# Reading the moving operand of every main matmul as two halves in turn

## The chip, the cores and the metric

The kernel runs on one core of a Trainium2 chip. The metric is the time of one execution on the device in microseconds (us). TensorE (PE) multiplies, VectorE (DVE) and ScalarE (ACT) do the elementwise work, GpSimd (POOL) a few small things, and SyncE (SP) issues nearly all DMAs. A matmul has a stationary operand, which is loaded into TensorE first (a row "PEld" of the profile), and a moving operand, which is streamed through it column by column; its result lands in PSUM, in banks of 512 fp32 columns.

## What is computed

One layer of a hybrid decoder on x of 512 tokens by 2048 features, all in float32:

```python
h    = rms_norm(x, norm1_g);  proj = h @ w_in          # 2048 -> 6160 columns
out_a = gla_mixer(...)        # 4 heads of chunked gated linear attention
out_b = dilated_mixer(...)    # 8 heads of dilated attention, three branches merged
x = x + concat(out_a, out_b) @ w_out                   # 2048 -> 2048
h2 = rms_norm(x, norm2_g)
x = x + (silu(h2 @ w_gate) * (h2 @ w_up)) @ w_down     # 2048 -> 5632 -> 2048
```

The five big products (w_in, w_out, w_gate, w_up, w_down) hold nearly all the work. The mixers are small beside them.

## The kernel before, in words

**The big products.** The work goes by pairs: one pair multiplies 512 tokens by two weight blocks of 512 columns each. A pair uses a Strassen-like scheme of seven products (P1, P5, P6, P3, P7, P2, P4 in `PRODUCTS`) in place of eight, each over a quarter of the weights, and each product runs over `groups` of 256 rows (four, or three in the last third of w_down). So a pair with four groups is 28 items. `stream` (L302) walks all items of 20 pairs as one list; `first_pair` (L369) does the same for the first pair with a hand-written order of side work (`FIRST`).

For each item a weight sum of 128 x 1024 is made by DVE where the product needs one (`source`, L245), and split into a high part `wh` (ACT, L315, rounded to the type fp32r) and a low part `wl` (DVE, L319, the rest, fp32r). The activations were split in the same way into `a[:, :, 0, :]` and `a[:, :, 1, :]` (L174, L175). The product is high x high, low x high and high x low, so an item has 12 matmuls: 8 with `wh` as moving operand, 4 with `wl` (L345; L413 in the first pair). Each matmul streams `w[:, jj, :]`, 512 fp32r columns that lie next to each other in one partition (2048 bytes), against 128 x 128 of `a`, and adds into one bank `acc`. Two slots each of `wh` and `wl` (`hpool`) let the split of item k+1 run while item k is multiplied.

**Moves out of PSUM.** A product that is complete is read out of `acc` by ACT into a `seed` tile (`seeds`, L269 without and L271 with a row scale), or added from `acc` to such a tile by DVE (`close`, L281 and L283). In the first pair the two are L427 and L437. The last quarter of a pair is read straight out of PSUM by the pair's final step: `emitted` (L536), `final_gate` (L1128 and L1134), `residual` (L1293) or the silu in `final_ffn` (L1408). All read 512 neighbouring columns and write 512 neighbouring columns. `later(1, ...)` and `later(2, ...)` put them one and two items behind the end of the product, in the middle of an item's matmuls.

**What sets the order.** PE, ACT and DVE take their instructions in the order in which the code above issues them. The mixers, the transposes (L1092) and the splits of activations are generators in `background`, from which `step` runs a few between the `wh` and the `wl` matmuls of an item. The weights come by DMAs of 512 KB from SP (L222) into 12 slots.

Of the kernel before, what the change touches and what calls it, by code (L numbers as in the profile page):

```python
# [13 lines left out]
AF = mybir.ActivationFunctionType  # L14
ALU = mybir.AluOpType
# [3 lines left out]
P = 128  # L19
# [88 lines left out]
def block_kernel(ctx: ExitStack, tc: tile.TileContext, ins, out):  # L108
    nc = tc.nc
# [109 lines left out]
    def load_quarter(rows, name, g, w):  # L219
# [2 lines left out]
        load(t, w[r0 : r0 + 256, :].rearrange("(j p) n -> p j n", p=P))  # L222
        return t

    class Pair:


# [35 lines left out]
        def seeds(self, src, half):  # L263
            res = []

            def one(m):
                t = cpool.tile([P, 512], F32, name=nm("seed"), tag="C")
                if self.scale is None:
                    nc.scalar.copy(t, src[m])  # L269
                else:  # L270
                    nc.scalar.activation(t, src[m], AF.Copy, scale=self.scale(half, m))  # L271
                res.append(t)

            later(1, lambda: one(0))
            later(2, lambda: one(1))
            return res

        def close(self, seed, src, half, which):
            def one(m):
                if self.scale is None:  # L280
                    nc.vector.tensor_tensor(seed[m], src[m], seed[m], op=ALU.add)  # L281
                else:
                    nc.vector.scalar_tensor_tensor(  # L283
                        seed[m], src[m], self.scale(half, m), seed[m], op0=ALU.mult, op1=ALU.add
                    )
                if m == 1:
                    self.final(half, which, seed, None)

            later(1, lambda: one(0))
            later(2, lambda: one(1))  # L290
# [11 lines left out]
    def stream(pairs):  # L302


        items = [(p, prod, g) for p in pairs for prod in PRODUCTS for g in range(p.op.groups)]
        last = len(items) - 1
        sources, high, low = {}, {}, {}

        def total(k):
            p, prod, g = items[k]  # L310
            sources[k] = p.source(prod, g)

        def first_part(k):
            high[k] = hpool.tile([P, 2, 512], F32R, name=nm("wh"), tag="wh")
            nc.scalar.copy(high[k], sources[k])  # L315

        def second_part(k):
            low[k] = hpool.tile([P, 2, 512], F32R, name=nm("wl"), tag="wl")
            nc.vector.tensor_tensor(  # L319
                low[k], sources.pop(k), high[k].bitcast(F32), op=ALU.subtract  # L320
            )

        total(0)
        first_part(0)
        total(1)
        second_part(0)
        for k, (p, prod, g) in enumerate(items):
            if g == 0:
                if prod == "P1" and p.before:
                    p.before()  # L330
                p.begin(prod)
            run_soon()
            if k < last:
                first_part(k + 1)
            if k + 2 <= last:
                total(k + 2)
            if k < last:
                second_part(k + 1)
            a = p.op.t[COMBO[prod], g]
            fresh = prod in ("P1", "P5", "P2")  # L340
            for w, terms in ((high.pop(k), (0, 1)), (low.pop(k), (0,))):
                for jj in range(2):
                    for m in range(2):
                        for hl in terms:
                            nc.tensor.matmul(  # L345
                                p.dst[prod][m], a[:, jj, hl, m * P : (m + 1) * P], w[:, jj, :],
                                start=fresh and g == 0 and len(terms) == 2 and jj == 0 and hl == 0,
                                stop=g == p.op.groups - 1 and len(terms) == 1 and jj == 1,
                                skip_group_check=not fresh,
                            )  # L350
                if len(terms) == 2:
                    p.step()
            if g == p.op.groups - 1:
                p.end(prod)
# [14 lines left out]
    def first_pair(op, rows, w1, w2, final, unit, pre):  # L369
# [36 lines left out]
        def multiply(k, w, terms):  # L406
            prod, g = items[k]
            fresh = prod in ("P1", "P2", "P5", "P4")
            a = op.t[COMBO[prod], g]
            for jj in range(2):  # L410
                for m in range(2):
                    for hl in terms:
                        recent["pe"] = nc.tensor.matmul(  # L413
                            dst[prod][m], a[:, jj, hl, m * P : (m + 1) * P], w[:, jj, :],
                            start=fresh and g == 0 and len(terms) == 2 and jj == 0 and hl == 0,
                            stop=g == op.groups - 1 and len(terms) == 1 and jj == 1,
                            skip_group_check=not fresh,
                        ).ins

        seeds = {}  # L420

        def seed(name):
            prod, half = {"a": ("P1", 0), "b": ("P5", 1), "c": ("P1", 0), "d": ("P1", 1)}[name]
            seeds[name] = []
            for m in range(2):
                t = cpool.tile([P, 512], F32, name=nm("seed"), tag="C")
                recent["act"] = nc.scalar.activation(  # L427
                    t, dst[prod][m], AF.Copy, scale=row_scale(half, m)
                ).ins
                seeds[name].append(t)  # L430

        def close(name):
            prod, half, which = {
                "a": ("P2", 0, 0), "c": ("P5", 0, 1), "b": ("P1", 1, 1), "d": ("P4", 1, 0)
            }[name]
            for m in range(2):
                recent["dve"] = nc.vector.scalar_tensor_tensor(  # L437
                    seeds[name][m], dst[prod][m], row_scale(half, m), seeds[name][m],
                    op0=ALU.mult, op1=ALU.add,
                ).ins  # L440
            final(half, which, seeds[name], None)
# [89 lines left out]
    def emitted(c, scale):  # L531

        res = []
        for m in range(2):
            t = cpool.tile([P, 512], F32, name=nm("cout"), tag="C")
            nc.scalar.activation(t, c[m], AF.Copy, scale=scale(m))  # L536
            res.append(t)
        return res

# [115 lines left out]
    for what in LOADS.split():  # L655
        name, i = what[0], int(what[1])
# [461 lines left out]
    def final_gate(half, which, tiles, acc_):  # L1118
        og = onorm.pop((half, which))
        if tiles is None:  # L1120
            tiles = [cpool.tile([P, 512], F32, name=nm("cr"), tag="C") for _ in range(2)]
            src = acc_
        else:
            src = tiles
        for m in range(2):
            if src is acc_:
                nc.vector.scalar_tensor_tensor(
                    og[m], src[m], row_scale(half, m), og[m], op0=ALU.mult, op1=ALU.mult  # L1128
                )
                neg = nrs1[:, 2 * half + m : 2 * half + m + 1]  # L1130
            else:
                nc.vector.tensor_tensor(og[m], src[m], og[m], op=ALU.mult)
                neg = -1.0
            nc.scalar.activation(tiles[m], src[m], AF.Exp, scale=neg)  # L1134
            nc.scalar.activation(tiles[m], tiles[m], AF.Ln, bias=1.0)
            nc.scalar.activation(tiles[m], tiles[m], AF.Exp, scale=-1.0)

        def rest():
            for m in range(2):
                nc.vector.tensor_tensor(tiles[m], tiles[m], og[m], op=ALU.mult)  # L1140
            spare = apool.tile([P, 2, 2, 256], F32, name=nm("turned"), tag="A")
            later(1, lambda: transposed_store(
                tiles, half, mix_d[2 * which : 2 * which + 2], spare=spare
            ))

        soon(rest, 2)
# [141 lines left out]
    def residual(tiles, acc_, rest):  # L1288
        res = []
        for m in range(2):  # L1290
            r = rest[m]
            if tiles is None:
                nc.vector.tensor_tensor(r, acc_[m], r, op=ALU.add)  # L1293
                res.append(r)
            else:
                nc.vector.tensor_tensor(tiles[m], tiles[m], r, op=ALU.add)
                res.append(tiles[m])
        return res
# [98 lines left out]
    def final_ffn(j):  # L1397
        ups = {}

        def final(half, which, tiles, acc_):  # L1400
# [4 lines left out]
            for m in range(2):  # L1405
                if tiles is None:
                    s = work(("q", "k")[m])
                    nc.scalar.activation(s, acc_[m], AF.Silu, scale=tok_scale(half, m))  # L1408
                else:
                    s = tiles[m]  # L1410
                    nc.scalar.activation(s, s, AF.Silu)
                nc.vector.tensor_tensor(up[m], up[m], s, op=ALU.mult)
# [151 lines left out]
```

## Time and profile before

| what | us |
|---|---|
| median of 3 runs (2044.23 to 2045.43) | 2045.07 |
| the profiled execution | 2045.94 |
| its span, first to last instruction | 2044.1 |
| PE busy (9226 matmuls) | 2012.2 |
| DVE busy (1850 instructions) | 1657.6 |
| ACT busy (1600 instructions) | 1101.2 |
| POOL busy | 58.1 |

A row of the grouped view has the line of the kernel, the engine, the operation, output and inputs by the program's names, the shape and the count, then the busy time of the group in us and the mean of one instruction in ns, then the idle time of the engine just before them and what ended it. Busy times of matmuls overlap, since one starts before the one ahead has ended; so the mean of one matmul is not the distance between two.

### The profile page before, as it was taken

How to read it: one execution, taken by the hardware profiler on the slowest of the kernel's cores; microseconds unless marked ns; L12 is line 12 of the kernel's file. 1: busy time of each engine (PE TensorE's matmuls, PEld its weight loads, DVE VectorE, ACT ScalarE, POOL GpSimd, SP SyncE). 2: the span in 40 equal slices, each digit the busy share in tenths (PEclk: the TensorE clock that was granted, in tenths of full speed). 3: DMA queues.
4: the chain of work that ended last, by engine and by line, in shares of the span. 5: the costliest groups of instructions: out<-in, count | busy, mean ns of one | idle time of the engine just before them, and what ended most of it. 6: DMA issues, size and time to landing. Idle time of an engine off the chain costs nothing.

```text
span 2044.1 us, 25815 instructions
## 1 busy us (share of the span) xinstructions
PE 2012.2 (98%) x9226; PEld 1661.4 (81%) x9226; DVE 1657.6 (81%) x1850; ACT 1101.2 (54%) x1600; POOL 58.1 (3%) x81
## 2 busy tenths in 40 slices
PE   7999999999999999999999999999999999999999
PEld 6888888887877777888888888888888888888887
DVE  7997786768689889868868768778779979979977
ACT  7664464566675775544544444445446645546443
POOL 0000131011000000000000000000000000000000
PEclk9999999999999999999999999999999999999999
DMA  8347455454666684453453553543545855855662
GB/s 268 131 160 240 132 164 174 136 153 141 211 204 229 201 278 153 140 180 127 157 173 122 164 157 122 165 157 122 170 152 170 273 195 177 295 173 174 234 206 72
DMA packets 237113, 360.45 MB, mean 176 GB/s; under 512 B 18246, under 2 KB 96783, under 8 KB 236984
## 3 DMA queue, kind: packets, MB, share of 16 engines
q1 hardware_dynamic: 236776, 358.72, 54.0%
q8 instruction: 72, 1.18, 0.2%
q14 instruction: 57, 0.47, 0.1%
q10 hardware_dynamic: 208, 0.08, 0.0%
HBM read 296.59 MB, written 64.51 MB: 177 GB/s over the span
## 4 chain that ended last, share of the span: by engine, by line
PE 88%; DVE 5%; DMA 4%; issue 1%; ACT 1%; SPq 1%; POOL 0%; DVEq 0%; ACTq 0%; POOLq 0%
PE acc L345 79%; PE acc L413 3%; DVE wl L319 2%; PE bank L1092 1%; DVE wa L245 1%; PE bank L989 1%; PE bank L957 1%; DMA x<-in_x 1%; DVE AS L175 1%; PE bank L982 0%; DMA top<-mix_d 0%; DMA xn_d<-oT 0%; DMA wc<-in_w_in 0%; PE bank L413 0%; PE bank L742 0%
## 5 line engine op out<-in xcount | busy, mean ns | idle before, releaser
L345 PE MATMUL acc<-wh,AS 128*128 128x512 f32 x3008 | 745.1, 390 | 0.0
L345 PEld LDWEIGHTS acc<-wh,AS 128*128 128x128 f32 x3008 | 565.1, 188 | 118.6 <-ACT wh L315 0.3
L315 ACT CAST wh<-wa 128x1024 fp32r<-128x1024 f32 x376 | 395.9, 1053 | 453.3 <-PE acc L345 421.1
L345 PE MATMUL acc<-wh,AA 128*128 128x512 f32 x2256 | 558.0, 389 | 1.4 <-ACT wh L315 1.4
L319 DVE TENSOR_TENSOR wl<-wa,wh 128x1024 fp32r<-128x1024 f32 x376 | 458.2, 1220 | 105.0 <-ACT wh L315 64.9
L345 PEld LDWEIGHTS acc<-wh,AA 128*128 128x128 f32 x2256 | 423.2, 188 | 90.0 <-ACT wh L315 2.0
L345 PE MATMUL acc<-wl,AS 128*128 128x512 f32 x1504 | 410.3, 394 | 4.6 <-DVE wl L319 4.5
L345 PEld LDWEIGHTS acc<-wl,AS 128*128 128x128 f32 x1504 | 280.5, 188 | 67.5 <-DVE wl L319 8.5
L345 PE MATMUL acc<-wl,AA 128*128 128x512 f32 x1128 | 309.1, 395 | 2.0 <-DVE wl L319 2.0
L345 PEld LDWEIGHTS acc<-wl,AA 128*128 128x128 f32 x1128 | 209.1, 188 | 45.4 <-DVE wl L319 3.1
L315 ACT CAST wh<-wb 128x1024 fp32r<-128x1024 f32 x94 | 99.1, 1054 | 130.2 <-PE acc L345 123.4
L315 ACT CAST wh<-wc 128x1024 fp32r<-128x1024 f32 x94 | 99.0, 1053 | 127.8 <-PE acc L345 112.6
L315 ACT CAST wh<-wd 128x1024 fp32r<-128x1024 f32 x94 | 99.1, 1054 | 116.5 <-PE acc L345 111.6
L319 DVE TENSOR_TENSOR wl<-wc,wh 128x1024 fp32r<-128x1024 f32 x94 | 114.8, 1222 | 50.3 <-ACT wh L315 47.9
L319 DVE TENSOR_TENSOR wl<-wd,wh 128x1024 fp32r<-128x1024 f32 x94 | 114.7, 1221 | 47.9 <-ACT wh L315 40.7
L245 DVE TENSOR_TENSOR wa<-wc,wa 128x1024 f32<-128x1024 f32 x94 | 114.5, 1223 | 42.6 <-DMA wc<-in_w_gate 24.0
L319 DVE TENSOR_TENSOR wl<-wb,wh 128x1024 fp32r<-128x1024 f32 x94 | 114.4, 1219 | 10.7 <-ACT wh L315 10.2
L245 DVE TENSOR_TENSOR wb<-wd,wb 128x1024 f32<-128x1024 f32 x94 | 114.6, 1219 | 0.5
L245 DVE TENSOR_TENSOR wa<-wb,wa 128x1024 f32<-128x1024 f32 x94 | 113.7, 1220 | 0.8
L245 DVE TENSOR_TENSOR wa<-wd,wa 128x1024 f32<-128x1024 f32 x94 | 112.9, 1219 | 0.1
L283 DVE SCALAR_TENSOR_TENSOR seed<-acc,rs,seed 128x512 f32<-128x512 f32 x96 | 70.5, 747 | 29.5 <-PE acc L345 29.5
L271 ACT ACTIVATE seed<-acc,rs 128x512 f32<-128x512 f32 x96 | 60.6, 681 | 1.3 <-PE acc L345 1.2
(283 smaller groups left out, 1368.5 us busy)
## 6 DMA issues: line engine op xcount, KB each, us to landing
wa<-in_w_gate SPq DMA_DIRECT2D x44, 512.0 KB, 3.5
wb<-in_w_up SPq DMA_DIRECT2D x44, 512.0 KB, 4.3
wd<-in_w_up SPq DMA_DIRECT2D x44, 512.0 KB, 3.4
wc<-in_w_gate SPq DMA_DIRECT2D x44, 512.0 KB, 3.4
wc<-in_w_in SPq DMA_DIRECT2D x28, 512.0 KB, 3.8
wa<-in_w_in SPq DMA_DIRECT2D x24, 512.0 KB, 4.4
wb<-in_w_in SPq DMA_DIRECT2D x24, 512.0 KB, 6.0
wd<-in_w_in SPq DMA_DIRECT2D x24, 512.0 KB, 5.6
```

The source lines that it names most:

```text
L175: nc.vector.tensor_tensor(a[:, :, 1, :], src, a[:, :, 0, :].bitcast(F32), op=ALU.subtract)
L245: nc.vector.tensor_tensor(src, self.quarter(one, g), src, op=ALU.subtract)
L271: nc.scalar.activation(t, src[m], AF.Copy, scale=self.scale(half, m))
L283: nc.vector.scalar_tensor_tensor(seed[m], src[m], self.scale(half, m), seed[m], op0=ALU.mult, op1=ALU.add)
L315: nc.scalar.copy(high[k], sources[k])
L319: nc.vector.tensor_tensor(low[k], sources.pop(k), high[k].bitcast(F32), op=ALU.subtract)
L345: nc.tensor.matmul(p.dst[prod][m], a[:, jj, hl, m * P : (m + 1) * P], w[:, jj, :], start=fresh and g == 0 and len(terms) == 2 and jj == 0 ...
L413: recent["pe"] = nc.tensor.matmul(dst[prod][m], a[:, jj, hl, m * P : (m + 1) * P], w[:, jj, :], start=fresh and g == 0 and len(terms) == 2 ...
L957: nc.tensor.matmul(lp[:, :n], qh[:, b * P : (b + 1) * P], kh[:, :n], start=True, stop=True)
L989: nc.tensor.matmul(op, vh[:, k, :], lgs[b][:, k * P : (k + 1) * P], start=(k == 0), stop=(k == b))
L1092: nc.tensor.transpose(bk[:, jj, m * P : (m + 1) * P], tiles[m][:, f : f + P], ident)
```

## The change

Each main matmul gets its moving operand through a view that takes column 0 of the first half, column 0 of the second half (256 columns, 1024 bytes further on), column 1 of the first half, and so on. The matmul still writes 512 neighbouring columns of `acc`, which now hold the two halves interleaved. Each move out of `acc` reads it in steps of two columns, first the even ones, then the odd ones, and writes them as two halves, so that every tile in SBUF is what it was. In `final_gate` the Exp is issued apart for the case that reads PSUM and the case that reads SBUF; the instructions are the same. Nothing else is changed: transposes, the mixers' matmuls, `wh`, `wl`, `a` and all DMAs are as before.

```diff
+    def folded(w):
+        return w.rearrange("p (b a) -> p a b", b=2)
+    def unfolded(t):
+        return t.rearrange("p (a b) -> p b a", b=2)
+    def halves(t):
+        return t.rearrange("p (b a) -> p b a", b=2)
...
-                    nc.scalar.copy(t, src[m])
+                    nc.scalar.copy(halves(t), unfolded(src[m]))
                 else:
-                    nc.scalar.activation(t, src[m], AF.Copy, scale=self.scale(half, m))
+                    nc.scalar.activation(
+                        halves(t), unfolded(src[m]), AF.Copy, scale=self.scale(half, m)
+                    )
...
-                    nc.vector.tensor_tensor(seed[m], src[m], seed[m], op=ALU.add)
+                    nc.vector.tensor_tensor(
+                        halves(seed[m]), unfolded(src[m]), halves(seed[m]), op=ALU.add
+                    )
                 else:
                     nc.vector.scalar_tensor_tensor(
-                        seed[m], src[m], self.scale(half, m), seed[m], op0=ALU.mult, op1=ALU.add
+                        halves(seed[m]), unfolded(src[m]), self.scale(half, m), halves(seed[m]),
+                        op0=ALU.mult, op1=ALU.add,
                     )
...
                             nc.tensor.matmul(
-                                p.dst[prod][m], a[:, jj, hl, m * P : (m + 1) * P], w[:, jj, :],
+                                p.dst[prod][m], a[:, jj, hl, m * P : (m + 1) * P], folded(w[:, jj, :]),
...
-            nc.scalar.activation(t, c[m], AF.Copy, scale=scale(m))
+            nc.scalar.activation(halves(t), unfolded(c[m]), AF.Copy, scale=scale(m))
...
-                nc.vector.tensor_tensor(r, acc_[m], r, op=ALU.add)
+                nc.vector.tensor_tensor(halves(r), unfolded(acc_[m]), halves(r), op=ALU.add)
...
-                    nc.scalar.activation(s, acc_[m], AF.Silu, scale=tok_scale(half, m))
+                    nc.scalar.activation(
+                        halves(s), unfolded(acc_[m]), AF.Silu, scale=tok_scale(half, m)
+                    )
```

The matmul, the seed and the close of the first pair (L413, L427, L437) and the two reads of PSUM in `final_gate` (L1128, L1134) are changed in the same manner.

More of the change, by code (lines that the diff above doesn't have):

```diff
@@ L413, in multiply @@
                         recent["pe"] = nc.tensor.matmul(
-                            dst[prod][m], a[:, jj, hl, m * P : (m + 1) * P], w[:, jj, :],
+                            dst[prod][m], a[:, jj, hl, m * P : (m + 1) * P], folded(w[:, jj, :]),
                             start=fresh and g == 0 and len(terms) == 2 and jj == 0 and hl == 0,
@@ L427, in seed @@
                 recent["act"] = nc.scalar.activation(
-                    t, dst[prod][m], AF.Copy, scale=row_scale(half, m)
+                    halves(t), unfolded(dst[prod][m]), AF.Copy, scale=row_scale(half, m)
                 ).ins
@@ L437, in close @@
                 recent["dve"] = nc.vector.scalar_tensor_tensor(
-                    seeds[name][m], dst[prod][m], row_scale(half, m), seeds[name][m],
+                    halves(seeds[name][m]), unfolded(dst[prod][m]), row_scale(half, m),
+                    halves(seeds[name][m]),
                     op0=ALU.mult, op1=ALU.add,
@@ L1127, in final_gate @@
                 nc.vector.scalar_tensor_tensor(
-                    og[m], src[m], row_scale(half, m), og[m], op0=ALU.mult, op1=ALU.mult
+                    halves(og[m]), unfolded(src[m]), row_scale(half, m), halves(og[m]),
+                    op0=ALU.mult, op1=ALU.mult,
                 )
                 neg = nrs1[:, 2 * half + m : 2 * half + m + 1]
+                nc.scalar.activation(halves(tiles[m]), unfolded(src[m]), AF.Exp, scale=neg)
             else:
                 nc.vector.tensor_tensor(og[m], src[m], og[m], op=ALU.mult)
-                neg = -1.0
-            nc.scalar.activation(tiles[m], src[m], AF.Exp, scale=neg)
+                nc.scalar.activation(tiles[m], src[m], AF.Exp, scale=-1.0)
             nc.scalar.activation(tiles[m], tiles[m], AF.Ln, bias=1.0)
```

## The prediction

> **What bounds the kernel now.** I read the page first: the span, the busy shares, the granted clock.
>
> ```profile
> span 2044.1 us, 25815 instructions
> PE 2012.2 (98%) x9226; PEld 1661.4 (81%) x9226; DVE 1657.6 (81%) x1850; ACT 1101.2 (54%) x1600; POOL 58.1 (3%) x81
> PEclk9999999999999999999999999999999999999999
> PE 88%; DVE 5%; DMA 4%; issue 1%; ACT 1%; SPq 1%; POOL 0%; DVEq 0%; ACTq 0%; POOLq 0%
> ```
>
> The clock is full from end to end, and PE carries 88% of the chain that ended last. A busy PE need not be PE at its best, so I read next how far apart the main matmuls start: a piece of that chain (start, length, what) in the middle of the feed-forward part, and one pair of the same part by engine.
>
> ```profile
> 1315.71 65.30 PE acc L345 x288
> ...
> 1237.65:1315.71 78.06, 78.06 (x354) 64.66 (x353) 60.35 (x59) 37.28 (x43) 0.00 (x0) 1.00 0.46 149
> ```
>
> 288 matmuls of 512 columns in 65.30 us are **0.2267 us from start to start**. The second row (stretch, length, then busy time of PE, PEld, DVE, ACT, POOL, clock, DMA share, GB/s) has PE busy in all of its 78.06 us, DVE in 60.35, ACT in 37.28. PE's stream is the bound, and DVE has 17.7 us to spare per pair. The groups by form show how many matmuls the change touches, and how little PE waits ahead of them.
>
> ```profile
> L345 PE MATMUL acc<-wh,AS 128*128 128x512 f32 x3008 | 745.1, 390 | 0.0
> L345 PE MATMUL acc<-wh,AA 128*128 128x512 f32 x2256 | 558.0, 389 | 1.4 <-ACT wh L315 1.4
> L345 PE MATMUL acc<-wl,AS 128*128 128x512 f32 x1504 | 410.3, 394 | 4.6 <-DVE wl L319 4.5
> L345 PE MATMUL acc<-wl,AA 128*128 128x512 f32 x1128 | 309.1, 395 | 2.0 <-DVE wl L319 2.0
> ...
> L413 PE MATMUL acc<-wh,AS 128*128 128x512 f32 x128 | 31.6, 389 | 0.0
> L413 PE MATMUL acc<-wl,AS 128*128 128x512 f32 x64 | 17.1, 390 | 0.0
> L413 PE MATMUL acc<-wh,AA 128*128 128x512 f32 x64 | 16.0, 392 | 0.7 <-ACT wh L393 0.7
> ...
> L413 PE MATMUL bank<-wh,AA 128*128 128x512 f32 x32 | 9.3, 440 | 0.0
> L413 PE MATMUL acc<-wl,AA 128*128 128x512 f32 x32 | 9.0, 402 | 0.0
> L413 PE MATMUL bank<-wl,AA 128*128 128x512 f32 x16 | 4.8, 426 | 0.0
> ```
>
> That is 7896 of L345 and 336 of L413, **8232 matmuls**; at 0.2267 us they are 1866 us of the span. PE idles 8.0 us ahead of those of L345. So the price of this change is 8232 times what one matmul's start-to-start time changes by: each 10 ns is 82 us.
>
> **The change part by part.** Count and order of the instructions stay on every engine, so no queue is passed and no wait is added. Two things change: how a matmul reads its moving operand, and how 352 moves read PSUM.
>
> *The moving read.* No row of the trace has a moving operand whose neighbours in the stream are not neighbours in memory, so the cost is bounded from both sides. The nearest rows for a slower stream are fp32 matmuls of the same 512 columns (line 822): each call shows as two records, and their columns have the same four bytes as fp32r ones.
>
> ```profile
> 179.97 1.02 PE L822 MATMUL bank<-T,mats 128*128 128x512 f32 x2
> ...
> L822 PE MATMUL bank<-T,mats 128*128 128x512 f32 x8 | 4.1, 594 | 0.0
> ```
>
> The first row (start, length, count) has two of them in 1.02 us, and one takes 0.594; the second starts 1.02 - 0.594 = **0.426 us** behind the first. That is twice 0.213, so an fp32r stream runs at about two columns in the time of one fp32 column. I read this as two neighbouring columns being fetched at once, a supposition that fits the factor but that no row proves. If it holds, a stream whose next column lies 1024 bytes away gets one column per fetch. The start-to-start time is then 0.426 at the least (the fp32 rate), and twice 0.2267 = 0.453 at the most (all that a matmul costs now is doubled). Below, the bound is a stream with nothing lost, half of 0.426 = 0.213. I take the slow side, because the fp32 row is the only one in which four-byte columns come one at a time, and there the middle, 0.440:
>
> 8232 x (0.440 - 0.2267) = 1756 us more. The 8.0 us of idling of L345 go away, as wh and wl get nearly twice the time. From the profiled execution, 2045.94: 2045.94 + 1756 - 8 = **3794 us**. Its ends: 8232 x 0.1993 = 1641 gives 3679, and 8232 x 0.2267 = 1866 gives 3904. The profiled execution stands 0.9 us above the median of the runs; that is nothing here.
>
> [...]
>
> *The moves out of PSUM.* They are these groups, with rows for the price of a column behind them:
>
> ```profile
> L283 DVE SCALAR_TENSOR_TENSOR seed<-acc,rs,seed 128x512 f32<-128x512 f32 x96 | 70.5, 747 | 29.5 <-PE acc L345 29.5
> L271 ACT ACTIVATE seed<-acc,rs 128x512 f32<-128x512 f32 x96 | 60.6, 681 | 1.3 <-PE acc L345 1.2
> L281 DVE TENSOR_TENSOR seed<-acc,seed 128x512 f32<-128x512 f32 x48 | 32.4, 686 | 13.7 <-PE acc L345 13.7
> L269 ACT COPY seed<-acc 128x512 f32<-128x512 f32 x48 | 25.6, 585 | 0.0
> ...
> L962 DVE CUSTOM_DVE_ANT_0 L<-bank,T 128x512 f32<-128x512 f32 x4 | 2.7, 687 | 1.3 <-PE bank L957 1.3
> L962 DVE CUSTOM_DVE_ANT_0 L<-bank,T 128x256 f32<-128x256 f32 x4 | 1.7, 420 | 0.3 <-PE bank L957 0.3
> ...
> L992 ACT COPY r<-bank 128x128 f32<-128x128 f32 x16 | 4.2, 265 | 1.8 <-PE bank L989 1.7
> ```
>
> DVE has 96 + 48 of them plus 6 (L437), 16 (L1293) and 2 (L1128), 168; ACT has 96 + 48 plus 8 (L427), 8 (L536), 22 (L1408) and 2 (L1134), 184. No row reads PSUM in steps. Below, the cost is nothing. Above, I let each column cost twice: DVE pays (687 - 420) / 256 = 1.04 ns a column, 0.53 us for 512, and ACT (585 - 265) / 384 = 0.83 ns, 0.43 us; together 168 x 0.53 = 90 us on DVE and 184 x 0.43 = 78 us on ACT. A gain is excluded, as the same columns are moved. In the forecast all of it is hidden: at 0.440 an item of 12 matmuls takes 5.3 us where it took 2.7, and DVE kept up with the old one. I take nothing. If that cover is gone, because PE keeps its pace, the cost is the first rival's.
>
> *Banks.* A bank is read one or two items behind the end of its product and written again by PE a product later, some 28 matmuls or 6 us on; a move longer by 0.5 us fits in.
>
> **The rivals.**
>
> *PE keeps its pace (the interleaved read costs nothing).* Then the change does nothing to what bounds the kernel, and only the slower moves are left. The place is DVE's queue in an item that has a close, a split of activations and a sum besides `wl`: the next `wl` comes late, and PE waits.
>
> ```profile
> PEld acc L345 <- DVE wl L319: 11.6, 14, 1.9
> PE acc L345 <- DVE wl L319: 6.5, 9, 1.5
> 1627.00:2044.00 417.00, 412.14 (x1821) 341.11 (x1819) 354.95 (x373) 201.83 (x237) 0.00 (x0) 1.00 0.57 190
> ```
>
> Such waits are few now (18.1 us in 23 waits), but DVE is 85% busy in the last 417 us. Of the 90 us I let 0 to 40 come through: 2046 to 2086, with 2055 as its point. Against it speaks that fp32r needs twice the rate of fp32.
>
> *Faster.* A matmul takes 0.2267 where the doubled fp32 rate gives 0.213; 13.7 ns are lost each time. If they are lost where a contiguous read goes on to the next stretch of memory, two streams in turn may cover each other's change, provided both halves can be held open at once; from there on it decides. All gone: 8232 x 0.0137 = 113 us, 1933; half gone: 1989. I price it at 1960. Matmuls of 256 columns speak against it:
>
> ```profile
> 60.58 2.04 PE L742 MATMUL bank<-AS,gs 128*128 128x256 f32 x16
> ...
> L742 PE MATMUL bank<-AS,gs 128*128 128x256 f32 x16 | 2.0, 280 | 0.0
> ```
>
> 16 of them in 2.04 us, the last 0.280 long, are (2.04 - 0.28) / 15 = 0.117 apart, 10.8 ns over half of 0.213. A loss per column would be half of 13.7; this is most of it, so the loss looks more like one per matmul, which no order of columns removes. [...]
>
> *A rate between.* The read loses something, but part of the pairing survives or the two fetches overlap: 0.25 to 0.41 us, 2240 to 3550.
>
> *A quarter of the pace.* If a column from elsewhere takes not one but two fetch times, 0.88 us: 2045.94 + 8232 x 0.653 = 7420. Nothing in the trace asks for it; nothing excludes it.
>
> **How the numbers follow.**
>
> | case | us | chance |
> |---|---|---|
> | half the pace (forecast) | 3679 to 3904, 3794 | 0.48 |
> | PE keeps its pace | 2046 to 2086, 2055 | 0.14 |
> | faster | 1933 to 2040, 1960 | 0.18 |
> | a rate between | 2240 to 3550 | 0.11 |
> | a quarter of the pace | about 7420 | 0.09 |
>
> The predicted time is the forecast's, 3794. The likeliest case's own range is 3680 to 3905. Both signs have weight, so the range that should hold 8 in 10 reaches down to the faster case: 1945 to 3905; left out are the quarter pace and the outermost of the faster case and of the forecast. About 0.2% is what a measurement of this kernel can tell from no change (2041 to 2049): 0.05 of the 0.14 in which PE keeps its pace falls there. So faster 0.18, same 0.05, slower 0.77.
>
> **What would show it.** In the profile after, the piece of 288 matmuls in the chain should take 288 x 0.440 = 127 us, within 123 to 131, and the mean of one main matmul should rise from 390 ns to about 600, as the 594 of the fp32 row. ACT's wait of `wh` for PE should roughly double, DVE's share fall from 81% towards 45%, and PE's idling ahead of L345's successor vanish. L283's and L269's means tell the cost of the stepped read of PSUM, 747 and 585 if there is none, about 1280 and 1010 if each column costs double. The prediction is wrong if the 288 matmuls take 65 us or less: then the supposition that neighbours are fetched together is wrong, and the sign hangs on whether they take 61 to 62 us (the loss per matmul goes) or 65.3 with DVE late.

## The result, and the profile after

The changed kernel takes 1985.3 us (median of 4 runs, 1983.05 to 1986.54) against 2045.25 for the kernel before: a ratio of 0.970, 95% interval 0.9679 to 0.9721. It is **faster by 60 us**, where the forecast was 3794. From the page of the profile after:

```profile
span 1984.0 us, 25786 instructions
PE 1931.4 (97%) x9226; PEld 1672.0 (84%) x9226; DVE 1653.4 (83%) x1850; ACT 1096.3 (55%) x1600; POOL 62.4 (3%) x81
```

PE's busy time fell by 80.8 us; its idle time, span less busy, rose from 31.9 to 52.6 us, so 20.7 came back. The mean granted clock is 0.994 where it was 0.998. A piece of the chain of waits (start, length, what) and one feed-forward pair by engine:

```profile
1129.35 62.19 PE acc L361 x288
...
1129.35:1203.65 74.30, 74.30 (x353) 65.01 (x353) 60.19 (x59) 37.13 (x43) 0.00 (x0) 1.00 0.50 156
```

288 matmuls take 62.19 us where they took 65.30: **0.2159 us from start to start** in place of 0.2267. A pair is 74.30 us in place of 78.06, and DVE has 14.1 us to spare in it. The groups by form, two of the stream and the moves out of PSUM:

```profile
L361 PE MATMUL acc<-wh,AS 128*128 128x512 f32 x3008 | 714.0, 380 | 0.0
L361 PE MATMUL acc<-wh,AA 128*128 128x512 f32 x2256 | 536.0, 380 | 6.6 <-ACT wh L331 6.6
...
L298 DVE SCALAR_TENSOR_TENSOR seed<-acc,rs,seed 128x512 f32<-128x512 f32 x96 | 70.7, 749 | 24.7 <-PE acc L361 24.7
L282 ACT ACTIVATE seed<-acc,rs 128x512 f32<-128x512 f32 x96 | 60.8, 683 | 1.1 <-PE acc L361 1.0
L294 DVE TENSOR_TENSOR seed<-acc,seed 128x512 f32<-128x512 f32 x48 | 32.6, 692 | 11.7 <-PE acc L361 11.7
L280 ACT COPY seed<-acc 128x512 f32<-128x512 f32 x48 | 25.7, 589 | 0.0
```

The mean of a main matmul is 380 ns where it was 390 and 389. The moves out of PSUM take 749, 683, 692 and 589 ns where they took 747, 681, 686 and 585: the stepped read of PSUM costs under 1% in each of these groups.

So the sum is: 8232 x 10.8 ns = 89 us gained, 60 kept, 29 given back: 20.7 as idle time of PE, and some 8 because PE's busy time fell by 80.8 us and not by 89. Two questions were left: why a read that leaves its neighbours each time is faster, and where the 29 us went.

### The profile page after: what moved, and what is told of

It is laid out like the page before. It is cut to its first block, busy times and chain, and to the rows that moved or that the text cites. A ratio compares the mean times of both kernels' runs of the same rounds, so it can differ in the third digit from the quotient of the medians.

```text
span 1984.0 us, 25786 instructions
## 1 busy us (share of the span) xinstructions
PE 1931.4 (97%) x9226; PEld 1672.0 (84%) x9226; DVE 1653.4 (83%) x1850; ACT 1096.3 (55%) x1600; POOL 62.4 (3%) x81
## 4 chain that ended last, share of the span: by engine, by line
PE 83%; DVE 6%; DMA 6%; issue 2%; ACT 1%; SPq 1%; POOL 1%; DVEq 0%; ACTq 0%; POOLq 0%
PE acc L361 75%; PE acc L429 3%; DVE wl L335 2%; PE bank L1109 1%; DVE wa L256 1%; PE bank L1006 1%; PE bank L974 1%; DMA xn_d<-oT 1%; DMA x<-in_x 1%; ACT wh L331 1%; DMA x_d<-q 1%; DVE AS L175 1%; PE bank L999 0%; DMA wc<-in_w_in 0%; PE bank L759 0%
## 5 line engine op out<-in xcount | busy, mean ns | idle before, releaser
L361 PE MATMUL acc<-wh,AS 128*128 128x512 f32 x3008 | 714.0, 380 | 0.0
L361 PE MATMUL acc<-wh,AA 128*128 128x512 f32 x2256 | 536.0, 380 | 6.6 <-ACT wh L331 6.6
L361 PEld LDWEIGHTS acc<-wh,AA 128*128 128x128 f32 x2256 | 427.9, 190 | 68.6 <-ACT wh L331 7.8
L361 PE MATMUL acc<-wl,AS 128*128 128x512 f32 x1504 | 395.9, 385 | 7.9 <-DVE wl L335 7.8
L361 PE MATMUL acc<-wl,AA 128*128 128x512 f32 x1128 | 298.8, 387 | 3.6 <-DVE wl L335 3.4
```

Of the source, the lines that this page charges most:

```text
L361: nc.tensor.matmul(p.dst[prod][m], a[:, jj, hl, m * P : (m + 1) * P], folded(w[:, jj, :]), start=fresh and g == 0 and len(terms) == 2 and ...
```

## The experiments

### Which part does it: the reads alone, the moves alone

```diff
 # moves only: the changed kernel, but
-  ... a[:, jj, hl, m * P : (m + 1) * P], folded(w[:, jj, :]),
+  ... a[:, jj, hl, m * P : (m + 1) * P], w[:, jj, :],
 # reads only: the kernel before, but
-  ... a[:, jj, hl, m * P : (m + 1) * P], w[:, jj, :],
+  ... a[:, jj, hl, m * P : (m + 1) * P], folded(w[:, jj, :]),
```

> Only the moves out of PSUM are changed; the matmuls read neighbours, so the columns of what is moved come out permuted. If the gain is in the matmul's read: 2045, within 0.2% (L283 stayed at 747 to 749 ns in the profile after, so the stepped read of PSUM costs nothing). Rival, the gain is in the moves: 1985.

> Only the matmuls read the two halves in turn; the moves read neighbours, so the columns come out permuted. If the gain is in the matmul's read and the moves cost nothing: 1985, within 0.3% of the changed kernel. Rival, the moves give some of it back: 1975 or less. Rival, the gain is in the moves: 2045.

The moves alone: 2045.23 us, ratio 0.9997 (0.9988 to 1.0006), no change. The reads alone: 1980.13, ratio 0.9683 (0.9669 to 0.9698). The whole gain is in the matmuls' reads. To tell whether the reads alone are 5 us ahead of the whole change, both ran beside each other on one chip:

> The changed kernel once more, beside the next run on the same chip: 1983 to 1987.

> The reads alone once more (columns come out permuted): if the stepped moves out of PSUM cost something on the path, 4 to 6 us below the changed kernel, with intervals apart; if the first difference was scatter, within 2 us of it.

1981.82, ratio 0.9688 (0.967 to 0.9707), for the whole change and 1983.08, ratio 0.9686 (0.9671 to 0.9701), for the reads alone: the 5 us were scatter, and the stepped moves cost nothing that these runs can tell. The kernel before took 2046.52 us here, so the change is worth 64.7 us in this comparison and 60 in the first; the 29 us given back are 24 to 29.

### Is it any read that leaves its neighbours: steps of two

```diff
 def folded(w):
-    return w.rearrange("p (b a) -> p a b", b=2)   # column 0 of each half, column 1 of each half, ...
+    return w.rearrange("p (a b) -> p b a", b=2)   # columns 0, 2, 4, ..., then 1, 3, 5, ...
```

> As the run with the reads alone, but each matmul reads its even columns, then its odd ones (steps of two columns, 8 bytes); the columns come out permuted. Theory 'step': 1985, main matmuls 0.216 apart. Theory 'stretch': between 2030 and 2045, main matmuls 0.222 to 0.227 apart, since two sweeps of 256 pass over the same stretches one after the other.

3861.06 us, ratio 1.888 (1.8848 to 1.8911). Both theories named in the expectation fail. A piece of the chain:

```profile
1502.27 129.92 PE acc L349 x288
```

0.451 us from start to start. This is the half pace of the forecast, in size too (0.426 to 0.453), but for another order of the columns. Two orders, neither with a neighbour behind a neighbour, lie a factor of two apart (0.2159 and 0.451).

### The orders by themselves

A kernel that computes nothing of the layer and runs groups of 48 matmuls back to back, each line with its own order of the moving columns, for instance

```python
mm(o, stat(sr, i), wr[:, i // 4 % 2, :])                                      # L42, neighbours
mm(o, stat(sr, i), wr[:, i // 4 % 2, :].rearrange("p (b a) -> p a b", b=2))   # L43, halves in turn
```

> No part of the layer is computed: 24 groups of 48 matmuls, back to back, each group with its own order of the moving columns or its own type; read is the time from start to start. All theories: fp32r neighbours 0.227 us, two halves in turn 0.216. Theory 'stretch' (a contiguous fp32r read loses time at each new stretch of memory, and two streams far apart cover it): quarters and sixteenths in turn 0.216 too, halves 2048 bytes apart 0.216, but streams 2 or 16 columns apart, pairs or 16 columns in turn, and two runs of 256 neighbours stay at 0.220 to 0.227; a stationary operand with columns in steps of two changes nothing; 384 columns lose 10 ns (a share), not 13.7. Theory 'step' (what matters is only that the next column isn't the neighbour): every order whose next column is no neighbour gives 0.216, steps of two and the 2-column distance with it; runs and pairs stay near 0.227. Theory 'load' (the moving read collides with the load of the next stationary operand): stepped stationary columns change the 0.227, and 384 columns lose the full 13.7. fp32 and bf16 are not paired, or not limited by bytes: both orders alike, 0.43 a record and about 0.216. My old supposition (neighbours fetched together) would have had the halves at 0.43 or more and is out.

The timeline of PE (start, length, line, count); start to start is (length - mean of one) / 47, with the means from the second view. L42 is neighbours, L43 halves in turn, L44 quarters, L46 steps of two, L49 pairs of neighbours from each half in turn, L51 the order with distance 16 within blocks of 32, L52 the order 0,2,1,3, L54 two halves 2048 bytes apart; L61 and L62 are fp32 neighbours and halves, L63 and L64 bf16 neighbours and halves (the first record of L63 is missing from the trace, so its sum divides by 46).

```profile
19.41 11.04 PE L42 MATMUL bank<-wr,sr 128*128 128x512 f32 x48
30.29 10.52 PE L43 MATMUL bank<-wr,sr 128*128 128x512 f32 x48
40.65 13.75 PE L44 MATMUL bank<-wr,sr 128*128 128x512 f32 x48
...
75.08 21.85 PE L46 MATMUL bank<-wr,sr 128*128 128x512 f32 x48
...
139.70 16.50 PE L49 MATMUL bank<-wr,sr 128*128 128x512 f32 x48
...
167.56 10.52 PE L51 MATMUL bank<-wr,sr 128*128 128x512 f32 x48
177.92 11.05 PE L52 MATMUL bank<-wr,sr 128*128 128x512 f32 x48
...
199.69 10.52 PE L54 MATMUL bank<-wr,sr 128*128 128x512 f32 x48
210.05 11.36 PE L55 MATMUL bank<-wr,sr 128*128 128x512 f32 x48
...
258.86 41.37 PE L61 MATMUL bank<-w,s 128*128 128x512 f32 x96
300.06 52.00 PE L62 MATMUL bank<-w,s 128*128 128x512 f32 x96
352.12 10.31 PE L63 MATMUL bank<-wb,sbf 128*128 128x512 bf16 x47
362.26 23.41 PE L64 MATMUL bank<-wb,sbf 128*128 128x512 bf16 x48
```

```profile
L64 PE MATMUL bank<-wb,sbf 128*128 128x512 bf16 x48 | 23.4, 646 | 0.0
...
L46 PE MATMUL bank<-wr,sr 128*128 128x512 f32 x48 | 21.8, 633 | 0.0
...
L44 PE MATMUL bank<-wr,sr 128*128 128x512 f32 x48 | 13.7, 451 | 0.0
...
L42 PE MATMUL bank<-wr,sr 128*128 128x512 f32 x48 | 11.0, 389 | 0.0
...
L43 PE MATMUL bank<-wr,sr 128*128 128x512 f32 x48 | 10.5, 379 | 0.0
```

The kernel's own two times come out: (11.04 - 0.389) / 47 = 0.2266 for neighbours and (10.52 - 0.379) / 47 = 0.2158 for halves. Quarters are (13.75 - 0.451) / 47 = 0.283, steps of two (21.85 - 0.633) / 47 = 0.451; by the same sum pairs in turn are 0.340, and of the groups not shown here sixteenths are 0.435, 32 places in turn 0.433, steps of four 0.461, runs of 16 columns from each half in turn 0.240, and two runs of 256 one behind the other 0.227. Distance 16 and the halves 2048 bytes apart are as fast as the halves; 0,2,1,3 is as slow as neighbours. fp32 and bf16 **lose** by the same halves: 0.429 to 0.540 a record, and 0.216 to (23.41 - 0.646) / 47 = 0.484. So "stretch" falls (distance 16 should not have helped, quarters should have), and "step" falls (steps of two). Stepped stationary columns (L55) raise the neighbours' time to 0.233 and leave the halves at 0.216, as "load" had it; its other sign, that 384 columns lose the full 13.7 ns, did not come (11.5).

What fits these fp32r rows is a picture inferred from the times alone; no row of a trace shows a reader. The stream runs as if it were fetched by **two readers, one for the columns in even places of the order, one for those in odd places**, and as if what counts were how each reader's own columns lie. With halves in turn, one reader would get columns 0, 1, 2, ... and the other 256, 257, 258, ..., each a contiguous stream (0.2158). With neighbours each would get every second column (0.2266), with steps of two every fourth (0.451). With quarters and with pairs in turn each would jump between two places (0.283 and 0.340). fp32 and bf16 fit it with one reader, which jumps already with halves (0.540 and 0.484). The picture says which orders are slower; how much a jump costs (0.283, 0.340, 0.435) it doesn't say.

### The two readers put to a test

> No part of the layer is computed: 23 groups of 48 matmuls as in the first bench. New theory 'two readers': an fp32r stream is fetched by two readers, one for the columns in even places of the order and one for those in odd places, and what counts is how near together in memory each reader's own columns are; the next stationary operand's load gets in the way of readers that skip. It expects for fp32r: distance 2 (order 0,2,1,3) 0.227 as neighbours, distance 4 and 8 0.216, since each reader then gets 4 or 8 neighbours in a row; the quarters in another order (0,256,128,384) 0.283 as the quarters before, eight in turn slower than 0.283; runs of 4 in turn between 0.240 and 0.340; each column read twice (0,0,1,1) 0.216. [...] For the load: with 64 stationary columns the loss of neighbours, 10.8 ns over halves, falls to some 5, with 32 to some 3, halves stay at 0.216; with stationary columns in steps of four the neighbours lose more than the 17.4 of steps of two, halves nothing. Rival 'fixed loss': 10.8 whatever the stationary operand. [...]

L50 is distance 4 (0,4,1,5,...), L51 distance 8, L52 the quarters in another order, L53 eight in turn, L54 runs of four in turn, L55 each column twice; L56 and L58 are neighbours with 64 and 32 stationary columns, L59 and L60 neighbours and halves with stationary columns in steps of four.

```profile
52.14 10.52 PE L50 MATMUL bank<-wr,sr 128*128 128x512 f32 x48
62.50 10.52 PE L51 MATMUL bank<-wr,sr 128*128 128x512 f32 x48
72.86 13.75 PE L52 MATMUL bank<-wr,sr 128*128 128x512 f32 x48
86.44 23.56 PE L53 MATMUL bank<-wr,sr 128*128 128x512 f32 x48
109.80 12.20 PE L54 MATMUL bank<-wr,sr 128*128 128x512 f32 x48
121.84 10.52 PE L55 MATMUL bank<-wr,sr 128*128 128x512 f32 x48
132.20 11.21 PE L56 MATMUL bank<-wr,sr 128*64 128x512 f32 x48
...
153.60 11.28 PE L58 MATMUL bank<-wr,sr 128*32 128x512 f32 x48
164.72 11.44 PE L59 MATMUL bank<-wr,sr 128*128 128x512 f32 x48
176.00 11.59 PE L60 MATMUL bank<-wr,sr 128*128 128x512 f32 x48
```

Against the 10.52 us of halves, 11.04 of neighbours and 13.75 of quarters, all six orders came out as the two readers had it: distance 4 and 8 and each column twice at the time of halves, the quarters in another order at that of quarters, eight in turn above it, runs of four between halves and quarters (12.20, about 0.251 a matmul). The second part of the expectation failed. Loading 64 or 32 stationary columns in place of 128 doesn't shrink what neighbours lose (11.21 and 11.28), and with stationary columns in steps of four the neighbours lose more, as expected (11.44), but the halves lose as well (11.59).

The same bench has fp32 and bf16 in other orders. In fp32 the order 0,2,1,3 takes 0.429 us a record like its neighbours, and 0,4,1,5 takes 0.543; in bf16 the order 0,4,1,5 takes 0.216 like its neighbours, and distance 16 takes 0.482. The sizes agree with the picture, if these types have one reader. Steps of two lose 4.9% in fp32 (0.450 against 0.429) and 4.6% in bf16 (0.2258 against 0.2159); neighbours in fp32r, by this picture two readers in steps of two, lose 5.0% (0.2266 against 0.2158). fp32 in steps of four takes 2.10 times its neighbours' time (0.90 against 0.429), and fp32r in steps of two takes 2.09 times that of halves (0.451 against 0.2158). Not explained is that eight places in turn (L53, 0.487) are slower than sixteen (0.435).

### What the 10.8 ns are

> No part of the layer is computed: 20 groups of 48 fp32r matmuls, nearly all with neighbours as moving columns, to find what the 10.8 ns are that neighbours lose against halves. Theory 'fixed per matmul, a collision of the moving read with the load of the next stationary operand': 448 and 320 columns lose 10 to 11 ns against their halves as 512 did; the loss moves between 5 and 20 ns with the start of the stationary operand in memory (0, 1, 2, 4, 16, 32, 64 columns on), and falls when fewer stationary columns are loaded from the same start. Rival 'share of the columns': 448 columns lose 9.4, 320 lose 6.7. Rival 'fixed, but not the load': the start and the number of stationary columns change nothing.

L42 is neighbours, L46 the same with the stationary operand 4 columns further on, L49 64 further on; L56 and L57 neighbours and halves of 448 columns, L58 and L59 of 320; L60 is halves with the stationary operand 32 columns on.

```profile
19.51 11.04 PE L42 MATMUL bank<-wr,sr 128*128 128x512 f32 x48
...
63.51 11.36 PE L46 MATMUL bank<-wr,sr 128*128 128x512 f32 x48
...
97.07 11.05 PE L49 MATMUL bank<-wr,sr 128*128 128x512 f32 x48
...
173.69 10.07 PE L56 MATMUL bank<-wr,sr 128*128 128x448 f32 x48
183.60 9.24 PE L57 MATMUL bank<-wr,sr 128*128 128x448 f32 x48
192.68 7.20 PE L58 MATMUL bank<-wr,sr 128*128 128x320 f32 x48
199.71 6.68 PE L59 MATMUL bank<-wr,sr 128*128 128x320 f32 x48
206.23 10.52 PE L60 MATMUL bank<-wr,sr 128*128 128x512 f32 x48
```

Over 48 matmuls neighbours lose 0.52 us against halves at 512 and at 320 columns and 0.83 at 448; in the first bench they lose 0.39 at 256 columns and 0.55 at 384. That is 8 to 17 ns per matmul, neither a share of the columns nor one fixed amount, so "share" falls, and "fixed" holds at 320, 384 and 512 columns only. The loss depends on where the stationary operand starts (11.04 to 11.36), and halves are the same at the one other start tried. It depends as well on where the moving columns start: 508 columns from the third one on lose 0.77 us against their halves. The first two speak for a collision with the load of the next stationary operand, as "load" had it; that fewer loaded columns don't lower the loss speaks against it. Shown is that halves of 512 columns don't pay it, with the stationary columns contiguous or in steps of two (10.52 us both). That steps of two lose about the same 5% in fp32 and bf16 (4.9% and 4.6%) makes it likely, by the picture of the two readers, that it is the price of such steps; why it is paid, and why it changes with length and start, was not shown.

### Where the 29 us went

The subtractions that make the weight sums are left out of both kernels; the matmuls run on single quarters.

```diff
-            nc.vector.tensor_tensor(src, self.quarter(one, g), src, op=ALU.subtract)
+            self.quarter(one, g)
...
-            tt(sources[k], q[one, g], sources[k], op=ALU.subtract)
```

> The kernel before without the 376 + 16 subtractions that make the weight sums (they are left out; the matmuls run on single quarters), so DVE has some 475 us less to do. Its waits of PE for wl and wh (27 us over the pace in the stream) mostly vanish: 2015 to 2035.

> The changed kernel without the same subtractions. Theory 'given back by late engines' (8232 x 10.8 ns = 89 us were gained and some 25 to 30 given back because DVE and ACT, with DVE 83% busy, hand over wl and wh late): the difference to the kernel before without them is 80 to 90 us, so 1930 to 1950. Rival 'given back elsewhere' (transfers, the ends of the stream): the difference stays at 60 to 70.

2038.78 us (ratio 0.9962, 0.995 to 0.9973) without the change and 1955.75 (0.9559, 0.9543 to 0.9575) with it, both above what was expected, and **83.0 us apart** in place of 60 to 65. So with DVE relieved 18 to 23 us more are kept, and "given back elsewhere" falls. What PE itself waited for (us, times, longest), after the change with all work and without the sums:

```profile
PE acc L361 <- DVE wl L335: 11.2, 15, 2.1
PE bank L1109 <- ACT L L1322: 9.8, 6, 4.1
PE acc L361 <- ACT wh L331: 6.6, 3, 3.1
```

```profile
PE acc L361 <- ACT wh L331: 6.2, 2, 3.2
...
PE acc L361 <- DVE wl L335: 0.4, 1, 0.4
```

In the kernel before, the first three were 6.5, 4.3 and 1.4 us; they make 15.4 of the 20.7 us by which PE's idle time rose. Without the sums the wait for `wl` is gone and that of the transposes (L1109, L1108 without the sums) for ACT's `L` falls to 4.9 us; the wait for `wh` stays. In the kernel before, leaving out the sums took the wait for `wl` from 6.5 to 0.3 us but raised that for `wh` from 1.4 to 5.2, and so it gained 7 us and not the 10 to 30 expected.

The other part, some 8 us, is put down to PE working more slowly behind a wait (start, length, what; in brackets the idle time ahead of it and what ended it):

```profile
1848.02 0.62 ACT L174 CAST AA<-T 128x512 fp32r<-128x512 f32 x1 [6.52 <-DMA T<-p_d]
...
1849.64 3.78 PE L361 MATMUL acc<-wh,AA 128*128 128x512 f32 x8 [3.06 <-ACT wh L331]
```

Eight matmuls at the full pace take 7 x 0.2159 + 0.379 = 1.89 us; these take 3.78, and the granted clock from 1850 to 1860 us is 0.72. The trace after has seven waits of PE of 1.8 us or more behind its first 60 us, and behind four of them (2.1 to 4.1 us long) the matmuls run at about half pace for 2 to 4 us. The kernel before has one such wait, 1.9 us long and slow behind it too. In the pair without the sums PE's busy time differs by 88.0 us, nearly all of the 89.

A version of the changed kernel that issues the operands' loads earlier:

```diff
-        return staged(items, 2)          # both places
+        return staged(items, 3)
...
-                r = work(("T", "v")[m])  # first_columns: two places ahead, on two sets of tiles
+                r = work((("T", "v"), ("qT", "kT"))[i % 2][m])
```

> The changed kernel with the loads of operand parts issued one item earlier (three ahead in place of two) and the loads of the first columns two places ahead on other tiles. If the waits of ACT for such loads (T<-p_d 12.1 us, T<-x_d 5.3 us) are part of what was given back: 1965 to 1980. If they are not on the path: 1985. If the earlier loads collide with the weights' loads: 1990 or more.

1986.14, ratio 0.9709 (0.9691 to 0.9726): no gain. But the waits are hardly shorter either: T<-p_d 10.3 us where it was 12.1, and T<-x_d 7.2 where it was 5.3. So the run doesn't show what they cost. That they can reach the path is in the rows above: ACT waited 6.52 us for T<-p_d, made `wh` late by it, and PE idled 3.06 us.

### A version without stepped moves

The halves can also be read in turn if the split writes them so: even columns into the first half of `wh` and `wl`, odd ones into the second.

```diff
-            nc.scalar.copy(high[k], sources[k])
+            nc.scalar.copy(halves(high[k]), evens_odds(sources[k]))
...
-                low[k], sources.pop(k), high[k].bitcast(F32), op=ALU.subtract
+                halves(low[k]), evens_odds(sources.pop(k)), halves(high[k]).bitcast(F32), op=ALU.subtract
```

> A version without stepped moves: the split writes wh and wl with even columns in the first half and odd ones in the second (ACT and DVE read the weights in steps of two), so the halves read in turn give the natural order. If stepped reads of SBUF cost ACT and DVE nothing: as the reads alone, 1978 to 1983, and it beats the changed kernel. If each column costs double, ACT's cast of 1.05 us becomes 1.9 and DVE's 1.22 becomes 2.3, and DVE bounds an item: 2300 or more.

2078.31 us, ratio 1.0156 (1.0142 to 1.017), slower than both kernels and between the two cases expected. Where PE doesn't wait, the matmuls still start 0.216 apart, but:

```profile
L325 ACT CAST wh<-wa 128x1024 fp32r<-128x1024 f32 x376 | 577.9, 1539 | 284.4 <-PE acc L355 214.7 <-DVE wl L329 56.9 <-DVE wa L255 4.6
...
L329 DVE TENSOR_TENSOR wl<-wa,wh 128x1024 fp32r<-128x1024 f32 x376 | 556.0, 1483 | 69.8 <-ACT wh L325 42.6 <-PE acc L355 13.7 <-ACT oT L1110 13.1
...
PE acc L355 <- DVE wl L329: 59.6, 112, 2.3
```

The stepped read of SBUF costs ACT 1539 ns in place of 1053 and DVE 1483 in place of 1220, and PE idles 59.6 us for `wl`. The changed kernel stays the best that was found.

## Why the prediction was wrong

**What bounds the kernel** was right: 8232 matmuls at their start-to-start time, each 10 ns worth 82 us. The measured 10.8 ns are 89 us by it, and the two light kernels, 83 us apart, show the rule at work where DVE isn't in the way. The sign that the prediction had named for being wrong came too: the 288 matmuls take 62.19 us, less than 65.

**The step that failed** is "the moving read": "I read this as two neighbouring columns being fetched at once, ... a stream whose next column lies 1024 bytes away gets one column per fetch", priced at 0.440 us. In its place stands 0.2159. The fp32 row was a good measure of a stream at half pace, and such streams exist: steps of two take 0.451, and the kernel with them 3861 us. But the supposition took fp32's slower rate for a matter of neighbours. From the factor of two between fp32r and fp32 it follows only that two columns come in the time of one, not that they must be neighbours. Two readers with a stream each, the picture inferred above, would give the same factor, and the orders in which each has neighbours of its own in a row are the fast ones (0.2158). The prediction never asked for which orders the two would differ.

**The faster rival** had the right sign, and its price of 1960 was 25 us off. Its mechanism ("lost where a contiguous read goes on to the next stretch") was wrong: distance 4 does as well as 1024 bytes (10.52 us for 48 both). The argument held against it, from the 256-column matmuls, that the loss is not a share of the columns, was right (0.52 us per 48 at 512 and at 320 columns, 0.39 at 256); the conclusion "which no order of columns removes" was not: halves remove 10.8 of the 13.7 ns.

**The moves out of PSUM** were right in the sum, nothing, but for another reason than the one given: they were not hidden behind a slower PE, they did not get longer (747 to 749 ns). **"DVE late"**, named for the rival in which PE keeps its pace, came in the faster case, where 18 to 23 of the 89 us hang on DVE's work. The 18.1 us given there for such waits add the 11.6 us of the weight loads to PE's own 6.5; only the 6.5 are idle time of PE. That the granted clock is lower behind some of the longer waits (0.72 to 0.84 over 10 us) was in no case of the prediction, which read the clock as full from end to end.

The chance of 0.18 for faster was too low for what the trace had: one row at twice the fp32 rate, and no row at all of an order other than contiguous.

## What to carry to other kernels

In these runs an fp32r matmul stream took 0.2159 us per 512 columns with halves in turn and with distances of 4, 8 and 16 columns, orders whose even and odd places each take four neighbours or more in a row; it took 0.2267 with plain neighbours and 0.451 in steps of two. bf16 and fp32 lost by the halves (0.484 against 0.216, 0.540 against 0.429). The order was undone at under 1% of a move's time (747 to 749 ns) where results leave PSUM, but not in SBUF, where a step of two cost 0.26 to 0.49 us per 1024 columns. When the bounding engine becomes 5% faster, look at once at the engine that feeds it: here 24 to 29 of the 89 us gained went back in waits for DVE and ACT and in the slower matmuls behind the longer waits.

## What was not expected of the hardware

- Reading each column twice in a row (0,0,1,1) is as fast as the halves, 10.52 us for 48.
- fp32 in steps of two is (43.36 - 0.6) / 95 = 0.450 a record against 0.429, in steps of four 0.90:

```profile
280.78 43.36 PE L63 MATMUL bank<-w,s 128*128 128x512 f32 x96
323.98 86.56 PE L64 MATMUL bank<-w,s 128*128 128x512 f32 x96
```

- PSUM was read in steps of two by ACT and DVE at next to no cost (at most 6 ns in 686), while the same step in SBUF cost ACT 46% (1053 to 1539 ns) and DVE 22% (1220 to 1483 ns).
- Behind four of the six waits of PE of 2 us or more in the stream of the changed kernel the matmuls ran at about half pace for 2 to 4 us, with the granted clock over 10 us at 0.83, 0.84, 0.83 and 0.72 (from 524, 661, 755 and 1850 us); behind the other two (2.04 and 2.35 us long) it was 1.00.
